# First stage of a two-block transformer kernel: modulation products ahead of the transpositions, and ring slots in the order of the loads

## The chip, the cores and the metric

One core of a Trainium2 chip runs the whole kernel. The metric is the device time of one execution in microseconds (us). TensorE is the matrix engine, VectorE (DVE) and ScalarE (ACT) are the vector and activation engines, GpSimd (POOL) is the general one, SyncE (SP) issues nearly all the loads. Each engine runs its own instructions in the order in which the program issues them, and waits on semaphores for the others.

## What is computed

Two transformer blocks on 256 tokens of 1024 features. What matters here is the beginning of the first block:

```
c_act = silu(c)
mod = c_act @ w_ada + b_ada                 # six vectors of 1024: sh_m, sc_m, gt_m, sh_f, sc_f, gt_f
h = rmsnorm(x, g) * (1 + sc_m) + sh_m
q, k, v, f_logit, u = split(h @ w_in)       # 512, 512, 512, 8 and 512 columns
log_f = log_sigmoid(f_logit + b_fgate)      # forget gates of 8 heads
x = x + gt_m * (concat(attention(q, k, v, log_f), pool(u)) @ w_out)
```

A router and 32 experts follow, of which each token uses two, and then a second block with other attention branches and a feed-forward layer.

## The kernel before

**Weights.** All weights stream from HBM as tiles of 1 MB (128 rows of 2048 float32) through a ring of eleven slots, 0 to 3 in one pool and 4 to 10 in another (four more come later for the experts). A list, `plan` (line 173), names the tiles in the order in which they are loaded, with the slot of each: `a` are the eight tiles of the first two modulation vectors, `b` and `c` eight each of the next two pairs, `i` the eight of `w_in`, `o` the four of `w_out`. SP issues the loads in that order; a load waits until the last reader of its slot's previous tile is done. The experts' tiles follow with a list of their own, `slots` (line 669), and the second block's with four slots in turn (line 679).

**Three-pass products.** The projections are computed in three passes of float32r: each half tile of weights is split into an upper part `whi` by ScalarE (line 69) and a lower part `wlo` by VectorE (line 70), the activations into `hT` and `hL`, and `mmx` (line 129) issues upper x upper, upper x lower and lower x upper: lines 133, 134, 135. `next2` (line 90) hands out a half and has the following ones split, two ahead; there are three buffers for them.

**The first stage, in the order of the code.** The norm of x: ScalarE squares and sums the rows (line 241), VectorE adds epsilon (242), ScalarE and VectorE take the inverse root (231 to 235), and the rows are scaled, one block of tokens by VectorE (247), one by ScalarE (249). TensorE transposes them, 16 times 128 x 128 (line 264), into four PSUM tiles `ptr`.

Then `ada_first` (line 273) makes the first two modulation vectors, 128 columns of both from each `a` tile. For tile d: 8 products of silu(c), padded to 32 columns, with the weights into `pa` (line 282), each on a quarter of the columns of the array; a copy into `mr` by ScalarE (284); a product with ones that sums over the partitions (288); the bias by VectorE into `modT` (289). The sum of tile d - 1 is issued behind the products of tile d. After each tile, the loop at line 348 forms the gain `A1` (349) and evacuates transposed column d into `hT` and `hL` with gain and shift: for even d VectorE makes `evt` (341), ScalarE `hT` (342) and GpSimd `hL` (343); for odd d ScalarE makes `evt` (334), VectorE both parts (335, 336).

After the eighth tile the first two halves of `i0` are split (351), the gate logits `pf` are formed in 24 passes (lines 364 to 366), and the key products follow: `feat` (381), four of them, each of 24 passes into `pp`. ScalarE and VectorE turn `pf` into cumulated log gates meanwhile (367 to 379). Behind the fourth key product comes the first step of `ada_next` (293), which makes the next modulation vectors tile by tile between the other products (`some`, line 389): four products on half of the columns (line 301) on TensorE, the other half on VectorE (303, 305). Values, queries, attention, pooling, output projection and router follow.

The order is written by hand: the program issues exactly in the order of the code.

## Time and profile before

| | us |
|---|---|
| three runs | 771.41, 778.97, 775.15 |
| median of the runs | 775.15 |
| span of the profiled execution, first to last instruction | 772.4 |
| TensorE busy in it | 695.8 (90%) |
| VectorE, ScalarE, GpSimd busy | 400.1, 305.2, 136.2 |
| DMA engines' mean | 269 GB/s over the span, 207.7 MB |

The profile gives no time of its own for the profiled execution besides the span. Times in the rows count from the span's first instruction. A row of a timeline stands for one instruction or for several alike in a row (x count): start, length, engine, line, operation, output and inputs, shape, and in brackets how long the engine was idle before and what ended that.

### The profile page before, as it was taken

What the parts mean: (1) busy time and instruction counts of PE and PEld (TensorE: products, weight loads), DVE (VectorE), ACT (ScalarE), POOL (GpSimd) and SP (SyncE); (2) the same over time, 40 slices, a digit from 0 to 9 for tenths busy, and PEclk for the clock granted to TensorE, in tenths of its full rate; (3) what the DMA queues carried; (4) which work ended last, traced back from release to release, by engine and by line L of the source; (5) the groups of instructions that cost most, each with busy time, mean ns of one, the idle gap of its engine ahead of it and who ended that gap; (6) DMA issues with size and microseconds to landing.
All of it is one profiled execution on the core that took longest, in us unless ns stands there. A gap on an engine that the chain in (4) does not pass through costs nothing.

```text
span 772.4 us, 12245 instructions
## 1 busy us (share of the span) xinstructions
PE 695.8 (90%) x4953; PEld 532.0 (69%) x4953; DVE 400.1 (52%) x661; ACT 305.2 (40%) x531; POOL 136.2 (18%) x137
## 2 busy tenths in 40 slices
PE   3899999679988778767889999999999999999996
PEld 2687777544433132231489999999989998989885
DVE  2666796511221020120598878677867654545545
ACT  3643543310010000000466456686555554545433
POOL 0102321000000000000322343221422540503201
PEclk9999999889998897998999999999999999999998
DMA  9998499849999999999855433335545555545511
GB/s 359 419 419 359 173 347 422 339 149 424 420 421 422 420 421 422 421 420 421 320 202 191 145 142 127 110 134 193 180 192 188 191 206 171 204 170 190 192 55 55
DMA packets 29726, 207.70 MB, mean 269 GB/s; under 512 B 3553, under 2 KB 3937, under 8 KB 4706
## 3 DMA queue, kind: packets, MB, share of 16 engines
q1 hardware_dynamic: 29520, 206.35, 68.2%
q8 instruction: 41, 0.67, 0.4%
q10 hardware_dynamic: 146, 0.53, 0.2%
q14 instruction: 19, 0.16, 0.1%
HBM read 205.81 MB, written 1.05 MB: 268 GB/s over the span
## 4 chain that ended last, share of the span: by engine, by line
PE 57%; DMA 19%; DVE 2%; issue 0%; DVEq 0%; ACT 0%; SPq 0%; ACTq 0%
DMA w<-in_w_gu 14%; PE pp L133 9%; PE pp L134 9%; PE pp L135 9%; PE fy L133 4%; PE fy L135 4%; PE fy L134 4%; DMA w<-in_w_in 3%; DMA w<-in_w_dn 3%; PE pgu L895 3%; PE pg L775 2%; PE pB L1226 2%; PE y L853 1%; PE pd L928 1%; PE pv L133 1%; PE pv L134 1%
## 5 line engine op out<-in xcount | busy, mean ns | idle before, releaser
L70 DVE TENSOR_TENSOR wlo<-w,whi 128x1024 fp32r<-128x1024 f32 x144 | 182.4, 1270 | 100.3 <-ACT whi L69 99.4
L69 ACT ACTIVATE whi<-w 128x1024 fp32r<-128x1024 f32 x146 | 153.4, 1055 | 81.5 <-PE fy L135 41.5
L134 PE MATMUL pp<-hL,whi 128*128 128x256 f32 x368 | 103.5, 281 | 2.6 <-DVE hL L882 2.6
L133 PE MATMUL pp<-hT,whi 128*128 128x256 f32 x368 | 105.5, 287 | 0.0
L895 PE MATMUL pgu<-w,hg 128*32 128x512 f32 x512 | 72.4, 672 | 35.7 <-DMA w<-in_w_gu 31.4
L135 PE MATMUL pp<-hT,wlo 128*128 128x256 f32 x368 | 103.5, 281 | 0.5 <-DVE wlo L70 0.5
L895 PEld LDWEIGHTS pgu<-w,hg 128*32 128x32 f32 x512 | 14.0, 115 | 88.6 <-issue 46.8
L133 PEld LDWEIGHTS pp<-hT,whi 128*128 128x128 f32 x368 | 69.6, 189 | 3.8 <-issue 3.0
L133 PE MATMUL pp<-nH,whi 128*128 128x256 f32 x256 | 71.8, 281 | 0.0
L134 PE MATMUL pp<-nL,whi 128*128 128x256 f32 x256 | 71.7, 280 | 0.0
L135 PE MATMUL pp<-nH,wlo 128*128 128x256 f32 x256 | 71.7, 280 | 0.0
L134 PEld LDWEIGHTS pp<-hL,whi 128*128 128x128 f32 x368 | 69.6, 189 | 2.8 <-POOL wlo L70 2.8
L135 PEld LDWEIGHTS pp<-hT,wlo 128*128 128x128 f32 x368 | 69.6, 189 | 0.7 <-DVE wlo L70 0.7
L903 DVE TENSOR_TENSOR act<-pgu,act 128x256 f32<-128x256 f32 x8 | 3.4, 425 | 121.3 <-ACT act L902 121.3
L1504 POOL TENSOR_TENSOR aL<-rs,aH 128x256 fp32r<-128x256 f32 x32 | 46.3, 1446 | 89.5 <-ACT aH L1503 83.4
L902 ACT ACTIVATE act<-pgu 128x256 f32<-128x256 f32 x8 | 3.1, 384 | 142.7 <-PE pgu L895 142.7
L133 PE MATMUL fy<-whi,aH 128*128 128x512 f32 x124 | 49.3, 398 | 0.0
L134 PE MATMUL fy<-wlo,aH 128*128 128x512 f32 x124 | 48.8, 394 | 0.0
L135 PE MATMUL fy<-whi,aL 128*128 128x512 f32 x124 | 48.8, 394 | 0.0
L133 PEld LDWEIGHTS pp<-nH,whi 128*128 128x128 f32 x256 | 48.2, 188 | 0.1
L134 PEld LDWEIGHTS pp<-nL,whi 128*128 128x128 f32 x256 | 48.2, 188 | 0.1
L135 PEld LDWEIGHTS pp<-nH,wlo 128*128 128x128 f32 x256 | 48.2, 188 | 0.0
(427 smaller groups left out, 1299.0 us busy)
## 6 DMA issues: line engine op xcount, KB each, us to landing
w<-in_w_gu SPq DMA_DIRECT2D x64, 1024.0 KB, 19.8
w<-in_w_dn SPq DMA_DIRECT2D x32, 1024.0 KB, 19.8
w<-in_w_ff SPq DMA_DIRECT2D x32, 1024.0 KB, 4.8
w<-in_w_in SPq DMA_DIRECT2D x30, 1024.0 KB, 5.0
w<-in_w_ada SPq DMA_DIRECT2D x24, 1024.0 KB, 11.7
w<-in_w_out SPq DMA_DIRECT2D x8, 1024.0 KB, 4.7
w<-in_w_o SPq DMA_DIRECT2D x4, 1024.0 KB, 4.8
xt<-in_x SPq DMA_DIRECT2D x1, 1024.0 KB, 5.1
```

The costliest lines, as they stand in the source:

```text
L69: nc.scalar.activation(hi, w, AF.Copy)
L70: low = lambda e, lo=lo, w=w, hi=hi: e.tensor_tensor(lo, w, hi.bitcast(F32), op=OP.subtract)
L133: mm(out_, l[0], r[0], start=start, stop=False)
L134: mm(out_, l[0], r[1], start=False, stop=False)
L135: mm(out_, l[1], r[0], start=False, stop=stop)
L775: mm(pg[:, d], xn[:, t, 512 * b + 128 * d:512 * b + 128 * d + 128], Pf[:, t], start=(t == 0), stop=(t == 1))
L853: mm(pacc[t][h], pw[g][:, 128 * t:128 * t + 128], o, start=False, stop=(g == 7))
L895: mm(pgu[32 * j:32 * j + 32], hg[g][:, k, 32 * j:32 * j + 32], w[:, 512 * j:512 * j + 512], start=(k == 0), stop=(k == 7))
L903: V.tensor_tensor(act, pgu[:, 256:512], act, op=OP.mult)
L928: mm(pd[32 * j:32 * j + 32], aT[:, f, 32 * j:32 * j + 32], w[:, 512 * j:512 * j + 512], start=(f == 0), stop=(f == 1))
L1226: mm(p[:, 4 * t + h], kt[:, h, 128 * t:128 * t + 128], qo[:, h, n * t:n * t + n], start=True, stop=True)
L1504: G.tensor_tensor(aL[:, f], s, aH[:, f].bitcast(F32), op=OP.subtract)
```

## The change

1. The order of the first stage. Products and sum of modulation tile 0 stand ahead of the norm of x, those of tile 1 behind it and ahead of the transpositions. For each tile the sum now stands behind its own products. Tiles 2 to 6 have three of the gate's passes between their products and their sum; the two halves of `i0` are split behind column 6; tile 7 has four of the first key product's eight steps there. Its other steps, the second key product and the last gate passes follow. The copy of tiles 0 and 1 goes from ScalarE to VectorE.
2. `pf` gets another PSUM buffer (that of the later scores), so that it can be accumulated over the rounds.
3. The order of the loads and the slots. `i` tiles alternate with `b` and `c` tiles, and tile n goes to slot n % 11; the experts' tiles go on in the same count, and the second block's take slots 0 to 3 in order.

The diff without the comments that it removes, without the removed `ada_first` and without the lines that only move:

```
-    plan = "a0-7 0-7 i0-4 0-4 b0-3 5-8 i5 9 b4 10 b5 5 i6 6 b6-7 7-8 c0 0 i7 1 c1-2 2-3 o0 8 c3 10 c4 5 c5 7 o1 0 c6 4 c7 2 o2 3 o3 10"
+    plan = "a0 a1 a2 a3 a4 a5 a6 i0 a7 i1 i2 b0 b1 i3 b2 b3 i4 b4 b5 i5 b6 b7 i6 c0 c1 i7 c2 c3 c4 c5 o0 c6 o1 c7 o2 o3".split()
...
+    for n, what in enumerate(plan):
         w, split = src[what[0]]
-        for i, slot in zip(span(what[1:]), span(where)):
-            st.add(w[i], split, slot)
+        st.add(w[int(what[1:])], split, n % 11)
...
+    def ada_tile(d):
+        w = st.next()
+        pa = ps.tile([128, 512], F32, name="pa", tag="m", bufs=2)
+        for k in (0, 2, 4, 6, 1, 3, 5, 7):
+            j = 32 * (k // 2)
+            mm(pa[j:j + 32, 0:256], cs[:, k, :], w[:, 256 * k:256 * k + 256], start=(k % 2 == 0), stop=(k % 2 == 1))
+        mr = q1.tile([128, 256], F32, name="mr", bufs=2)
+        if d < 2:
+            V.tensor_copy(mr, pa[:, 0:256])
+        else:
+            S.activation(mr, pa[:, 0:256], AF.Copy)
+        return pa, mr
+    def ada_sum(d, pa, mr):
+        for j in range(2):
+            mm(pa[:, 256 + j:257 + j], mr[:, 128 * j:128 * j + 128], ones, start=True, stop=True)
+        V.tensor_tensor(modT[:, 0:2, d], pa[:, 256:258], vec[:, V_BA + d:V_BA + 16:8], op=OP.add)
...
+    ada_sum(0, *ada_tile(0))
     wfh = q1.tile([128, 8, 8], F32R, name="wfh")
...
+    rms_scale(r1, xt, q1, xn)
+    for t in range(2):
+        scale_rows(xn, xt, r1, t)
...
-    for d, _ in enumerate(ada_first()):
+    pf = ps.tile([128, 256], F32, name="pf", tag="s", bufs=2)
+    def f_logits(k):
+        mmx(pf[0:8], (wfh[:, k], wfl[:, k]), (hT[:, k], hL[:, k]), start=(k == 0), stop=(k == 7))
+    def column(d):
         V.scalar_tensor_tensor(A1[:, d:d + 1], mod(1)[:, d:d + 1], 1.0, vec[:, V_GM + d:V_GM + d + 1], op0=OP.add, op1=OP.mult)
         evac_split(q1, xT[d], hT[:, d], hL[:, d], A1[:, d:d + 1], mod(0)[:, d:d + 1], v=d % 2)
+    ada_sum(1, *ada_tile(1))
+    xT = transposed(ps, "a", xn)
+    column(0)
+    column(1)
+    for d in range(2, 7):
+        t = ada_tile(d)
+        f_logits(d - 2)
+        ada_sum(d, *t)
+        column(d)
+    st.split_to(2)
+    t = ada_tile(7)
+    kw = [st.next2(False) for _ in range(2)]
+    kp = [ps.tile([128, 256], F32, name="pp", tag="a", bufs=4) for _ in range(2)]
+    def k_part(i, k0, k1):
+        for k in range(k0, k1):
+            mmx(kp[i], sub(kw[i], slice(None), slice(128 * k, 128 * k + 128)), (hT[:, k], hL[:, k]), start=(k == 0), stop=(k == 7))
+    k_part(0, 0, 4)
+    ada_sum(7, *t)
+    column(7)
+    k_part(0, 4, 7)
+    k_part(1, 0, 7)
+    for k in (5, 6, 7):
+        f_logits(k)
+    for i in range(2):
+        k_part(i, 7, 8)
     st.split_to(LOOK)
...
-    for i in range(4):
+    for i in range(2):
+        S.activation(kT[:, i], kp[i], AF.Copy)
+    for i in range(2, 4):
         feat(st.next2(), kT[:, i])
...
-    slots = [9, 5, 7, 6, 4, 2, 1, 8, 0, 3, 10]
+    slots = [(n_pre + n) % 11 for n in range(11)]
...
-            st.add(a[name][i], True, (0, 3, 2, 1)[n % 4])
+            st.add(a[name][i], True, n % 4)
```

TensorE's first instructions before (`pa` with `cs` are a modulation tile's products, `pa` with `ones` its sums, `ptr` the transpositions):

```order
L264 MATMUL ptr<-ident,xn 128x128 x16
L282 MATMUL pa<-w_169,cs 32x256 x8
L282 MATMUL pa<-w_182,cs 32x256 x8
L288 MATMUL pa<-ones,mr 128x1 x2
L282 MATMUL pa<-w_203,cs 32x256 x8
L288 MATMUL pa<-ones,mr 128x1 x2
```

and now:

```order
L265 MATMUL pa<-w_127,cs 32x256 x8
L275 MATMUL pa<-ones,mr 128x1 x2
L265 MATMUL pa<-w_166,cs 32x256 x8
L275 MATMUL pa<-ones,mr 128x1 x2
L252 MATMUL ptr<-ident,xn 128x128 x16
L265 MATMUL pa<-w_212,cs 32x256 x8
L133 MATMUL pf<-hT,wfh 8x256
L134 MATMUL pf<-hL,wfh 8x256
L135 MATMUL pf<-hT,wfl 8x256
L275 MATMUL pa<-ones,mr 128x1 x2
```

Two tiles moved ahead of the transpositions, and a tile's sums from behind the next tile's products to behind its own and three gate passes.

VectorE around the start of the norm, now (`ss` is the sum of squares to which epsilon is added; before, the row with `ss` stood directly behind the lower bounds `olb`):

```order
L216 TENSOR_SCALAR olb<-lb 128x4
L268 COPY mr<-pa 128x256
L276 TENSOR_TENSOR modT<-pa,vec 128x2
L311 CAST wfh<-wf 128x64
L312 TENSOR_TENSOR wfl<-wf,wfh 128x64
L236 TENSOR_SCALAR ss<-ss 128x2
```

Four instructions moved ahead of the norm's first one on VectorE.

ScalarE at the first split of weights, before (`hT` and `evt` belong to columns 6 and 7, `w_337` is tile `i0`):

```order
L284 ACTIVATE mr<-pa 128x256
L342 ACTIVATE hT<-evt 128x256
L334 ACTIVATE evt<-ptr,modT,A_166 128x256
L69 ACTIVATE whi<-w_337 128x1024 x2
L368 ACTIVATE fz<-pf,vec 8x256
```

and now (`w_332` is `i0`, `w_422` is `i1`):

```order
L329 ACTIVATE hT<-evt 128x256
L69 ACTIVATE whi<-w_332 128x1024 x2
L270 ACTIVATE mr<-pa 128x256
L321 ACTIVATE evt<-ptr,modT,A_162 128x256
L69 ACTIVATE whi<-w_422 128x1024 x2
L393 ACTIVATE fz<-pf,vec 8x256
```

The split of `i0` moved from behind the last column to between column 6 and the copy of the eighth modulation tile.

## Rows read from the trace of the kernel before

**Rows 1.** Busy time by stretch: start:end, length, engines' busy us, clock, DMA share, GB/s.
```profile
46.20:147.00 100.80, 98.91 (x737) 76.82 (x736) 69.48 (x114) 40.88 (x90) 19.07 (x38) 1.00 0.82 331
164.00:376.00 212.00, 172.06 (x1090) 65.50 (x1093) 34.58 (x82) 18.07 (x42) 0.00 (x0) 0.90 1.00 413
...
76.00:87.00 11.00, 11.00 (x90) 8.32 (x91) 9.40 (x21) 5.08 (x14) 5.16 (x13) 1.00 0.01 1
157.00:166.00 9.00, 4.71 (x34) 2.86 (x36) 2.29 (x7) 2.79 (x5) 0.00 (x0) 0.87 0.03 6
```
**Rows 2.** TensorE's waits from 10 to 170: total us, times, longest.
```profile
PE ptr L264 <- DVE xn L247: 12.1, 1, 12.1
PE pa L282 <- DVE modT L289: 1.8, 6, 0.3
```
**Rows 3.** Timeline of TensorE: transpositions, modulation products and sums.
```profile
12.15 3.86 PE L264 MATMUL ptr<-ident,xn 128*128 128x128 f32 x16 [12.15 <-DVE xn L247]
15.93 2.41 PE L282 MATMUL pa<-w,cs 128*32 128x256 f32 x32
20.20 0.61 PE L288 MATMUL pa<-ones,mr 128*128 128x1 f32 x4
21.13 1.07 PE L282 MATMUL pa<-w,cs 128*32 128x256 f32 x16 [0.32 <-DVE modT L289]
22.99 1.07 PE L282 MATMUL pa<-w,cs 128*32 128x256 f32 x16 [0.26 <-DVE modT L289]
...
134.87 1.03 PE L593 MATMUL pn<-ident,xt 128*128 128x128 f32 x8
```
**Rows 4.** Timeline of the other engines in a round.
```profile
20.91 0.16 DVE L289 TENSOR_TENSOR modT<-pa,vec 128x2 f32<-128x2 f32 x1 [0.99 <-PE pa L288]
21.11 0.16 DVE L349 SCALAR_TENSOR_TENSOR A<-modT,vec 128x1 f32<-128x1 f32 x1
22.33 0.38 ACT L284 ACTIVATE mr<-pa 128x256 f32<-128x256 f32 x1 [0.46 <-PE pa L282]
23.17 0.54 DVE L341 TENSOR_SCALAR evt<-ptr,A,modT 128x256 f32<-128x256 f32 x1
23.75 0.42 ACT L342 ACTIVATE hT<-evt 128x256 fp32r<-128x256 f32 x1 [1.03 <-DVE evt L341]
```
**Rows 5.** Timeline of gate passes, split and first key product, and of the first b product.
```profile
30.82 0.28 PE L133 MATMUL pf<-hT,wfh 128*8 128x256 f32 x1
30.93 0.28 PE L134 MATMUL pf<-hL,wfh 128*8 128x256 f32 x1
32.19 2.00 ACT L69 ACTIVATE whi<-w 128x1024 fp32r<-128x1024 f32 x2
33.50 2.36 DVE L70 TENSOR_TENSOR wlo<-w,whi 128x1024 fp32r<-128x1024 f32 x2
34.78 0.39 PE L135 MATMUL pp<-hT,wlo 128*128 128x256 f32 x1 [0.50 <-DVE wlo L70]
35.00 0.28 PE L133 MATMUL pp<-hT,whi 128*128 128x256 f32 x1
35.12 0.29 PE L134 MATMUL pp<-hL,whi 128*128 128x256 f32 x1
...
46.24 0.64 PE L301 MATMUL pa<-w,cs 128*32 128x256 f32 x8
```
**Rows 6.** Loads of the first and the ninth tile: issue, and its time to landing.
```profile
2.86 4.89 SPq L50 DMA_DIRECT2D w<-in_w_ada  x8
DMA to landing us min/median/max: 6.5/6.5/6.5
17.55 0.33 SPq L50 DMA_DIRECT2D w<-in_w_in  x1
DMA to landing us min/median/max: 12.7/12.7/12.7
```
**Rows 7.** Timeline of VectorE at the start of the norm.
```profile
10.08 0.17 DVE L242 TENSOR_SCALAR ss<-ss 128x2 f32<-128x2 f32 x1 [1.30 <-ACT xn L241]
```

More of the change, by code (lines that the diff above doesn't have):

```diff
@@ L172, in body @@
     st.slots.update({i: ring if i < 4 else ring2 for i in range(11)})
-    plan = "a0-7 0-7 i0-4 0-4 b0-3 5-8 i5 9 b4 10 b5 5 i6 6 b6-7 7-8 c0 0 i7 1 c1-2 2-3 o0 8 c3 10 c4 5 c5 7 o1 0 c6 4 c7 2 o2 3 o3 10"
+    plan = "a0 a1 a2 a3 a4 a5 a6 i0 a7 i1 i2 b0 b1 i3 b2 b3 i4 b4 b5 i5 b6 b7 i6 c0 c1 i7 c2 c3 c4 c5 o0 c6 o1 c7 o2 o3".split()
     src = {"a": (a["w_ada"][0], 0), "b": (a["w_ada"][1], 0), "c": (a["w_ada"][2], 0), "i": (a["w_in"], 1), "o": (a["w_out"], 1)}
-    def span(x):
-        lo, _, hi = x.partition("-")
-        return range(int(lo), int(hi or lo) + 1)
-    plan = plan.split()
-    for what, where in zip(plan[::2], plan[1::2]):
+    for n, what in enumerate(plan):
         w, split = src[what[0]]
-        for i, slot in zip(span(what[1:]), span(where)):
-            st.add(w[i], split, slot)
+        st.add(w[int(what[1:])], split, n % 11)
     ones = cp.tile([128, 1], F32, name="ones")
@@ L249, in scale_rows @@
             S.activation(dst[:, t], src[:, t], AF.Copy, scale=r[:, t:t + 1])
-    xn = cp.tile([128, 2, 1024], F32, name="xn")
-    r1 = q1.tile([128, 2], F32, name="r1")
-    rms_scale(r1, xt, q1, xn)
-    for t in range(2):
-        scale_rows(xn, xt, r1, t)
     def transposed(ps, tag, src):
@@ L266, in transposed @@
         return r
-    xT = transposed(ps, "a", xn)
     modT = cp.tile([128, 6, 8], F32, name="modT")
-    def ada_first():
-        last = None
-        for d in range(9):
-            if d < 8:
-                w = st.next()
-                pa = ps.tile([128, 512], F32, name="pa", tag="m", bufs=2)
-                for k in (0, 2, 4, 6, 1, 3, 5, 7):
-                    j = 32 * (k // 2)
-                    mm(pa[j:j + 32, 0:256], cs[:, k, :], w[:, 256 * k:256 * k + 256], start=(k % 2 == 0), stop=(k % 2 == 1))
-                mr = q1.tile([128, 256], F32, name="mr", bufs=2)
-                S.activation(mr, pa[:, 0:256], AF.Copy)
-            if last:
-                pl, ml = last
-                for j in range(2):
-                    mm(pl[:, 256 + j:257 + j], ml[:, 128 * j:128 * j + 128], ones, start=True, stop=True)
-                V.tensor_tensor(modT[:, 0:2, d - 1], pl[:, 256:258], vec[:, V_BA + d - 1:V_BA + 16:8], op=OP.add)
-                yield
-            last = pa, mr
+    def ada_tile(d):
[14 more added lines that the diff above has]
+        V.tensor_tensor(modT[:, 0:2, d], pa[:, 256:258], vec[:, V_BA + d:V_BA + 16:8], op=OP.add)
     def ada_next(g):
@@ L343, in evac_split @@
             G.tensor_tensor(lo, t, hi.bitcast(F32), op=OP.subtract)
+    xn = cp.tile([128, 2, 1024], F32, name="xn")
+    r1 = q1.tile([128, 2], F32, name="r1")
+    rms_scale(r1, xt, q1, xn)
+    for t in range(2):
+        scale_rows(xn, xt, r1, t)
     A1 = q1.tile([128, 8], F32, name="A1")
@@ L362, in body @@
     catL = q1.tile([128, 8, 256], F32R, name="catL")
-    pf = ps.tile([128, 256], F32, name="pf", tag="a", bufs=4)
-    for k in range(8):
-        mmx(pf[0:8], (wfh[:, k], wfl[:, k]), (hT[:, k], hL[:, k]), start=(k == 0), stop=(k == 7))
     fz = q1.tile([8, 256], F32, name="fz", tag="mr", bufs=2)
```

## The prediction

> **What bounds the kernel now.** I read the table of busy time by stretch first, then TensorE's waits, then the timeline of the first 47 us, then the loads. The table by stretch [rows 1] shows four stages with three different limits. From 46.2 to 147 us TensorE is busy 98.91 of 100.80 us: whatever comes to it earlier or later by some time ends earlier or later by that time. Then the router runs, a chain of small steps, until about 164. From 164 to 376 the 16 DMA engines are busy all the time (share 1.00, 413 GB/s): the experts run at the pace of their weights. What follows (not shown here) is TensorE again. Two rows of the same group tell how the stages hang together. From 76 to 87 the DMA engines do nothing (share 0.01) while TensorE is busy 11.00 of 11.00 us, so in the first stage the loads are ahead of their use. From 157 to 166 they do nothing again (0.03): all fifteen slots that can be filled ahead for the experts are full, and the next load waits until TensorE frees one. So the bandwidth-bound stage starts when TensorE starts it, and a shift of the first stage goes through to the end of the kernel undiminished, in either direction.
>
> Thus only one thing is to be worked out: when TensorE reaches a point from which the order is the same in both kernels. I take the first product with the b weights (line 301), after all four key products: 46.24 us [rows 5].
>
> TensorE's waits say what there is to gain before that point: 12.1 us ahead of the first transposition, 1.8 us in six pieces between modulation products [rows 2], 0.5 us ahead of the first key product [rows 5]. The first is the tempting one. Its end is not all gain: the first modulation weights land at 9.4 us (issued at 2.86, 6.5 us to landing) [rows 6].
>
> **The change part by part.** The work on TensorE is the same: 8 modulation products, 8 pairs of sums over partitions, 16 transpositions, 24 gate passes, the key products. What changes is who waits in front of whom.
>
> *Two modulation products ahead of the transpositions.* A tile's product takes 1.07 us and its two sums 0.61 us at full pace [rows 3]. Before about 17 us TensorE runs at about half: 16 transpositions take 3.86 us, while eight take 1.03 us later [rows 3]. At half pace the first tile's product is done at 9.4 + 2.1 = 11.5. Its copy is now VectorE's; no row shows that copy, so I bound it by ScalarE's 0.38 and by VectorE's 0.54 for a tile of this shape with a scale and bias [rows 4], and take 0.45: 12.1 with 0.1 on each crossing (the sum ends at 20.81, the next step starts at 20.91) [rows 3, 4]. The sums take 1.2 at half pace: 13.3. Now comes the catch: VectorE runs in order, and the norm of x stands behind this sum. The add of epsilon (line 242, before at 10.08) [rows 7] comes after the modulation add and the two small casts of the gate weights, at about 14.0 instead of 10.08, so the rows of x are scaled at 16.1 where it was 12.1. VectorE then copies the second product (0.45), TensorE sums it (0.9 at half pace), and only then transposes: start 17.4, before 12.15. That is 5.3 us later, for two tiles of work (about 3.4 us at full pace) done ahead. The third modulation product starts after 16 transpositions, at 20.6 if they run at half pace (16 x 0.21 = 3.4), at 18.9 if the clock has risen by then (1.7).
>
> *Five rounds in which the sum no longer lags.* Before, the sum of tile d - 1 stood behind the product of tile d, so that ScalarE's copy had a whole product as cover; a round took 22.99 - 21.13 = 1.86 us [rows 3]. Now the sum of tile d stands directly behind its own product with three gate passes (0.34 us) between. A round is product 1.07, crossing 0.1, copy 0.38, crossing 0.1, sum 0.45 until the next product may start: 2.1 us. After an even column it is more, for ScalarE also writes hT: from the sum's start 0.61, crossing 0.1, modT 0.16, A 0.16, evt 0.54, hT 0.42 and small gaps make 2.1 us [rows 3, 4], while the next copy wants ScalarE at 0.45 + 1.07 + 0.1 = 1.6; it starts 0.45 late, and that round takes 2.55. Five rounds: 2.1 + 2.55 + 2.1 + 2.55 + 2.1 = 11.4. The weights do not set this pace: at 420 GB/s a 1 MB tile takes 2.5 us, tile 6 lands long before its round, and tile 7, now one place later in the queue, lands at 30.2 (the ninth megabyte of weights did so before: 17.55 + 12.7) [rows 1, 6]. The eighth product may start at 18.9 + 11.4 = 30.3, or 32.0.
>
> *Key products in between.* The two halves of the first key tile are split on ScalarE and VectorE, 2.00 and 2.36 us for two [rows 5]. They are issued behind column 6 and ahead of the eighth tile's copy. ScalarE ends column 6 at 1.67 us after the eighth product may start; the upper part takes 1.05, the lower part 1.23 more: the third pass of the first key product can run at + 4.05. TensorE has 1.0 of product and two passes (0.24) until then and stands still for about 2.8 us, where it stood for 0.5 before [rows 5]. The remaining 46 passes at 0.12, one pair of sums (0.44) and nine gate passes at 0.11 (1.0) make 6.96, and so both products end at + 11.0. The eighth column's own way (ScalarE's copy, sum, evt, hT, hL) is hidden behind these passes; without that cover it would cost about 2 us. Products three and four (48 x 0.12 = 5.76) bring the b product to + 16.8.
>
> The sum: 18.9 + 11.4 + 16.8 = 47.1 with an early rise of the clock, 20.6 + 11.4 + 16.8 = 48.8 with a late one; before 46.24. So the change costs 0.85 to 2.55 us. I take the middle, + 1.7, since no row decides where the clock rises.
>
> *Slots and the order of loads.* With b and i tiles in alternation the i tiles land up to 10 us later than before (`i4` has four tiles more ahead of it, at 2.5 us), and the c and o tiles earlier. I cost both at nothing: TensorE's unbroken work covers it [rows 1], and counted at 2.5 us a tile, the later i tiles still land about 5 us ahead of their split (an estimate). If that cover were gone, one late tile would cost at most its 2.5 us. SP issues the same loads; a tile of the second block gets another slot, freed some microseconds later but still ahead of its turn in the queue: 0.
>
> The profiled execution's span is 772.4; the median of three runs is 775.15. The shift does not depend on what lies between them, so I add it to the median: 775.15 + 1.7 = 776.9 (the span would be 774.1).
>
> **The rivals.** *First, not slower.* If the rounds keep the old pace, the two tiles done ahead pay. With an early clock the change breaks even when 18.9 + 5 P + 16.8 = 46.24, that is at a round of P = 2.1 us; at the old 1.9 it gains 1.0 us: 774.1. For it speaks that ScalarE is little used between 17 and 31; against it that its copy needs 0.1 + 0.38 + 0.1 in each round and the cover is three passes. As worked out above, the rounds after odd columns come out at just that limit, the others above.
>
> *Second, slower than forecast.* TensorE stays at its lower level past the transpositions. By the row alone the rise came 4 to 5 us after TensorE's first product at 12.15, which is also 4 to 5 us after the beginning of its first unbroken work [rows 3]; the changed kernel pulls these apart, with the first product at 9.4 and unbroken work only from 16.6. Counted from the latter plus a round at half pace, the sum becomes about + 4.2: 779.3. It decides when the rise comes after 21 us. The Trainium skill ("TensorE: Matmul & The Clock Gate", Part 1) says that the low level is the default, that activity releases it, and that the moment is not tied to the kernel's start. By that rule scattered products would count for less than I give them in the middle, and the time would lie at or above 777.7, the late end of my sum; this trace, with its single unbroken start, agrees with either reading.
>
> *Third, the loads decide.* If the new order of slots is what matters, the idle DMA stretch at 76 to 87 closes and the kernel gains nothing from it, since nobody waits there: 775.2. Against a gain speaks that the only waits on loads are in the expert stage, whose start TensorE sets.
>
> **How the numbers follow.** Chances: 0.6 for the forecast (0.85 to 2.55 slower), 0.17 for the first rival, 0.15 for the second, 0.03 for the third, 0.05 for what I do not see. Runs of the kernel before lie within 3.8 us of their median; for a median of a few I allow 3 (an estimate). The furthest gain is TensorE without a break from the landing of tile 7: 30.2 + 1.07 + 5.76 + 0.44 + 1.0 + 5.76 = 44.2 at the b product, 2.0 earlier. So the range goes from 775.15 - 2.0 - 3 = 770.1 to 775.15 + 4.2 + 3 = 782.3. A measurement of this kernel tells about 1% (7.75 us) from no change. No case above reaches that by itself; slower gets 0.07 for the second rival with an unseen stall, faster 0.04, no change 0.89.
>
> **What would show it.** In the profile after: the first modulation product at 9.5 and the transpositions not at 12 but at 17; rounds of 2.1 and 2.5 us in alternation, ended by ScalarE's copy; a wait of some 2.8 us ahead of the third pass of the first key product on the lower part of the weights; the first b product between 47 and 49 us; no idle DMA at 76 to 87 and the same idle stretch ahead of the experts; from there on everything later by the same 1 to 3 us. I am wrong if the b product comes before 46 us, if TensorE waits for a load in the first stage, or if the difference grows or shrinks after 50 us.

## The result, and the profile after

The changed kernel takes 781.42 us in the median of 11 runs (777.70 to 784.33); 11 runs of the kernel before have a median of 773.42 (770.97 to 778.97). The ratio is 1.0091, interval [1.0072, 1.011]: 7 us slower by the ratio (0.0091 x 773.42), 8 by the medians, where 1.7 was forecast. The time lies inside the range given, near its upper end, and the sign was right; the size was not. The profiled execution took 779.16, its span is 777.3. (One execution each of e7 and c6 and two of e15, below, were longer than their kernel's others by hundreds of us; medians and counts are given without them.)

What bounds the kernel after? First the table by stretch, as [rows 1]; the sixth column is the granted clock, 1.00 for the upper level (2.4 GHz) and 0.50 for the lower (1.2 GHz). The bounds of the last three rows are set where the clock changes.

```profile
46.20:147.00 100.80, 99.30 (x732) 77.06 (x730) 72.68 (x120) 43.19 (x94) 19.01 (x38) 0.98 0.83 325
164.00:376.00 212.00, 167.31 (x1095) 66.67 (x1093) 35.99 (x87) 18.85 (x44) 0.00 (x0) 0.93 0.97 401
...
76.00:87.00 11.00, 11.00 (x88) 8.45 (x88) 8.11 (x18) 3.97 (x13) 5.12 (x11) 1.00 0.83 308
157.00:166.00 9.00, 5.55 (x36) 5.47 (x36) 4.98 (x27) 0.54 (x3) 0.00 (x0) 0.62 0.63 265
...
21.20:34.70 13.50, 10.89 (x121) 5.92 (x117) 5.12 (x18) 5.49 (x12) 2.53 (x6) 1.00 1.02 416
34.70:41.60 6.90, 6.15 (x29) 6.06 (x29) 3.77 (x7) 2.25 (x4) 0.00 (x0) 0.51 1.02 418
72.30:75.70 3.40, 3.40 (x19) 2.19 (x19) 1.98 (x4) 2.59 (x9) 0.00 (x0) 0.50 1.01 414
```

The reader is to see two rows that have no counterpart before, the last two: TensorE is busy nearly all the time, yet at half its clock, from 34.7 to 41.6 and again from 72.3 to 75.7. In the kernel before the column reads 1.00 from 17.0 to 46.2, and so it does from there to 147 [rows 1]. (Ahead of its first rise the column shows 1.00 too, though the transpositions run at half pace; that rise is read from durations.) The idle stretch of the DMA engines at 76 to 87 is closed (0.83 against 0.01), and nobody gains by it, since TensorE is busy 11.00 of 11.00 there in both.

TensorE's waits up to 60 us, as [rows 2]:

```profile
PE pa L265 <- DMA w<-in_w_ada: 8.8, 1, 8.8
PE pp L133 <- ACT whi L69: 1.6, 1, 1.6
PE pa L275 <- DVE mr L268: 1.6, 2, 1.0
PE pp L135 <- DVE wlo L70: 0.8, 1, 0.8
PE pa L275 <- ACT mr L270: 0.8, 2, 0.4
```

The wait of 12.1 for the norm has become one of 8.8 for the first load; the six small waits on `modT` are gone; new are 1.6 on VectorE's copies of tiles 0 and 1, 0.8 on ScalarE's copies in two of the rounds, and 1.6 on the upper part of the first key tile; the wait on its lower part has grown from 0.5 to 0.8. The same in TensorE's timeline, as [rows 3, 5] (lines of the changed kernel: 265 modulation products, 275 sums, 252 transpositions, 133 to 135 passes, 286 first b product, 470 first scores):

```profile
8.84 1.94 PE L265 MATMUL pa<-w,cs 128*32 128x256 f32 x16 [8.84 <-DMA w<-in_w_ada]
16.08 3.65 PE L252 MATMUL ptr<-ident,xn 128*128 128x128 f32 x16
19.66 1.74 PE L265 MATMUL pa<-w,cs 128*32 128x256 f32 x16
...
24.34 0.61 PE L275 MATMUL pa<-ones,mr 128*128 128x1 f32 x4 [0.38 <-ACT mr L270]
...
31.64 1.07 PE L265 MATMUL pa<-w,cs 128*32 128x256 f32 x16
34.28 0.39 PE L133 MATMUL pp<-hT,whi 128*128 128x256 f32 x1 [1.56 <-ACT whi L69]
35.54 0.58 PE L135 MATMUL pp<-hT,wlo 128*128 128x256 f32 x1 [0.75 <-DVE wlo L70]
36.13 0.42 PE L134 MATMUL pp<-hL,whi 128*128 128x256 f32 x1
36.35 0.42 PE L135 MATMUL pp<-hT,wlo 128*128 128x256 f32 x1
...
51.13 0.64 PE L286 MATMUL pa<-w,cs 128*32 128x256 f32 x8
...
52.30 0.38 PE L134 MATMUL pv<-wlo,hT 128*128 128x256 f32 x1 [0.21 <-DVE wlo L70]
...
69.57 0.48 PE L470 MATMUL s<-kT,qT 64*128 64x128 f32 x2 [0.47 <-ACT qT L410]
```

and the first scores in the kernel before:

```profile
64.20 0.48 PE L443 MATMUL s<-kT,qT 64*128 64x128 f32 x2 [0.48 <-ACT qT L385]
```

Behind the wait the key passes follow each other every 0.22 us (36.13 to 36.35), where they did every 0.12 before [rows 5]. The b product stands at 51.13, before at 46.24: + 4.9. Followed product by product, the shift is 5.4 at the first scores (69.57 against 64.20; the 0.5 arises at the first value product, which waits for its lower weights at 52.30), 6.8 behind the second stretch at the lower level, and still 6.8 at the first expert product (170.68 against 163.90). In the expert stage it shrinks to 5 in this execution (the first product behind it: 381.83 against 376.71).

The other engines, at the norm and around that wait, as [rows 5, 7]:

```profile
12.80 0.16 DVE L236 TENSOR_SCALAR ss<-ss 128x2 f32<-128x2 f32 x1
...
32.86 0.42 ACT L329 ACTIVATE hT<-evt 128x256 fp32r<-128x256 f32 x1 [1.81 <-DVE evt L328]
33.19 1.99 ACT L69 ACTIVATE whi<-w 128x1024 fp32r<-128x1024 f32 x2
34.26 2.36 DVE L70 TENSOR_TENSOR wlo<-w,whi 128x1024 fp32r<-128x1024 f32 x2 [1.43 <-ACT whi L69]
```

ScalarE stood for 1.81 us ahead of the split: column 6 stands in front of it in its order, and waits for VectorE.

### The profile page after: what moved, and what is told of

Same layout as the page of the kernel before. It is cut to its first block, busy times and chain, and to the rows that moved or that the text cites. A ratio compares the mean times of both kernels' runs of the same rounds, so it can differ in the third digit from the quotient of the medians.

```text
span 777.3 us, 12247 instructions
## 1 busy us (share of the span) xinstructions
PE 700.5 (90%) x4953; PEld 536.9 (69%) x4953; DVE 399.3 (51%) x663; ACT 303.2 (39%) x529; POOL 136.1 (18%) x137
## 3 DMA queue, kind: packets, MB, share of 16 engines
HBM read 205.81 MB, written 1.05 MB: 266 GB/s over the span
## 4 chain that ended last, share of the span: by engine, by line
PE 53%; DMA 23%; DVE 2%; issue 0%; ACT 0%; DVEq 0%; SPq 0%; ACTq 0%
DMA w<-in_w_gu 15%; PE pp L133 9%; PE pp L134 9%; PE pp L135 9%; DMA w<-in_w_dn 8%; PE fy L133 4%; PE fy L135 4%; PE fy L134 4%; PE pgu L922 2%; PE pB L1253 2%; PE pv L133 1%; PE pv L134 1%; PE pv L135 1%; PE acc L134 1%; PE acc L135 1%; PE acc L133 1%
## 5 line engine op out<-in xcount | busy, mean ns | idle before, releaser
L69 ACT ACTIVATE whi<-w 128x1024 fp32r<-128x1024 f32 x146 | 153.2, 1053 | 86.3 <-PE fy L135 41.6
L133 PE MATMUL pp<-hT,whi 128*128 128x256 f32 x368 | 107.4, 292 | 1.6 <-ACT whi L69 1.6
L134 PEld LDWEIGHTS pp<-hL,whi 128*128 128x128 f32 x368 | 71.2, 193 | 2.7 <-POOL wlo L70 2.7
L134 PE MATMUL pp<-nL,whi 128*128 128x256 f32 x256 | 71.8, 280 | 0.0
L135 PE MATMUL pp<-nH,wlo 128*128 128x256 f32 x256 | 71.8, 280 | 0.0
```

The source lines that it names most:

```text
L69: nc.scalar.activation(hi, w, AF.Copy)
L133: mm(out_, l[0], r[0], start=start, stop=False)
L134: mm(out_, l[0], r[1], start=False, stop=False)
L135: mm(out_, l[1], r[0], start=False, stop=stop)
```

## The experiments

The theory: the changed order costs some 2.5 us by its waits, and the rest because TensorE's clock falls behind the wait ahead of the key products. The rivals: the waits alone, and the new order of the loads. The kernels ran in five groups, each on one chip beside runs of the kernel before, with which their ratios are formed: e1 to e4; e5, e7, e8 and e11; e12 to e15; c1 to c4; c5 and c6.

**Loads alone, order alone.** e1 is the kernel before with only the new `plan`, `slots` and `n % 4`; e2 is the changed kernel with the old ones.

```
# e1, in the kernel before (e2 is the reverse edit in the changed kernel)
-    plan = "a0-7 0-7 i0-4 0-4 b0-3 5-8 ..."
+    plan = "a0 a1 a2 a3 a4 a5 a6 i0 a7 i1 i2 b0 ...".split()
...
-    slots = [9, 5, 7, 6, 4, 2, 1, 8, 0, 3, 10]
+    slots = [(n_pre + n) % 11 for n in range(11)]
...
-            st.add(a[name][i], True, (0, 3, 2, 1)[n % 4])
+            st.add(a[name][i], True, n % 4)
```

> The kernel before with only the new order of loads and the new slots (first stage, experts, second block); the order of the work is the old one. Theory clock (the order of the work makes TensorE wait ahead of the key products, and the fall of its clock behind that wait costs more than the wait) and rival waits (only the waiting itself costs): both expect no change, within 1.5 us of before, first b product at 46 to 46.5 us. Rival loads (a part of the loss is in the loads and slots): 2 us or more slower.

Measured: 777.11 (12 runs; before beside them 773.24), ratio 1.0045 [1.0027, 1.0062]: under the old order of work the new loads cost 3.5 us, which both the theory and the waits alone had excluded. TensorE's timeline and the clock of e1:

```profile
27.25 0.60 PE L281 MATMUL pa<-ones,mr 128*128 128x1 f32 x4
30.02 1.08 PE L275 MATMUL pa<-w,cs 128*32 128x256 f32 x8 [2.16 <-DMA w<-in_w_ada]
```

```profile
29.80:36.50 6.70, 6.48 (x38) 4.21 (x39) 2.66 (x8) 2.90 (x5) 1.08 (x4) 0.50 1.02 423
70.80:74.10 3.30, 3.30 (x19) 2.18 (x19) 1.98 (x4) 2.52 (x9) 0.00 (x0) 0.50 1.00 412
```

The eighth modulation tile, now behind `i0`, lands 2.2 us later; the old rounds are at it earlier and wait 2.16 us, and the clock falls in that wait. The b product stands at 50.05, + 3.8. So a second, quite different wait of 2 us is followed by two such falls.

> The changed kernel with the old order of loads and the old slots. Clock and waits: 6 to 9 us slower than before, as the changed kernel. Loads: 2 us or more faster than the changed kernel.

Measured: 779.23 (6 runs), 1.0076 [1.0046, 1.0106], overlapping the changed kernel's interval; the same waits of 1.6 and 0.8, the same falls (0.52 from 35.8 to 42.5, 0.54 from 73.4 to 76.7), and the b product at 51.74, no earlier than with the new loads (51.13). Under the new order of work no cost of the loads can be told, since the rounds come to the eighth tile only at 31.64; the two intervals still leave room for some us.

**The wait shortened, the wait filled.** e3 splits the first half of `i0` one round earlier. e4 leaves the wait and puts useless products into it.

```
# e3, in the changed kernel
     for d in range(2, 7):
         t = ada_tile(d)
+        if d == 6:
+            st.split_to(1)
         f_logits(d - 2)
# e4, in the changed kernel
+    dm = ps.tile([128, 256], F32, name="dm", tag="s", bufs=2)
+    for i in range(24):
+        mm(dm, hT[:, i % 4, 0:128], hT[:, i % 4], start=True, stop=True)
     k_part(0, 0, 4)
```

> The changed kernel with the first half of i0 split right behind the copy of the seventh modulation tile instead of behind column 6. The wait ahead of the first key product's passes (1.56 and 0.75 us) should shrink to 0.5 or less. Clock: TensorE keeps its upper level between 31 and 46 us, the first b product comes at 46 to 47.5 instead of 51.1, the whole is 1 to 4 us slower than before. Waits: only the wait goes, b product at 49 or later, 4 to 6 us slower than before.

Measured: 777.07 (12), 1.0042 [1.0024, 1.006]. The wait on the key tile is down to 0.17, but ScalarE's copy for the eighth sum is now late by 1.6 us; the lower level lasts from 36.6 to 39.9, half as long, and again from 70.7 to 74.0. The b product comes at 49.01, where the waits alone expected 49 or later and the clock 46 to 47.5, while the time is what the clock expected: since the wait was moved and not taken away, this run does not part the two.

> The changed kernel with 24 further products of 256 columns into an unused PSUM tile between the eighth modulation product and the first key product; nobody reads them. They take about 2.9 us and lie in the time in which TensorE waits for the split. Clock: the upper level is kept, the first b product comes at 48 to 49 instead of 51.1, the whole is 2 to 4 us faster than the changed kernel. Waits: no gain, b product at 51 to 51.5, time as the changed kernel or up to 0.5 us more.

Measured: 776.72 (12), 1.0050 [1.0029, 1.0072]. Stretches of e4, from the filled wait on:

```profile
31.40:36.20 4.80, 4.80 (x48) 4.20 (x49) 2.86 (x6) 2.58 (x4) 1.08 (x4) 1.00 1.05 426
36.20:46.20 10.00, 10.00 (x87) 9.77 (x86) 4.59 (x9) 4.82 (x10) 0.00 (x0) 1.00 1.01 415
46.20:147.00 100.80, 99.25 (x739) 77.25 (x739) 72.59 (x119) 41.76 (x89) 19.07 (x38) 1.00 0.83 326
```

No stretch below 1.00: with 24 products more the kernel is 3 to 5 us faster than the changed one (by the ratios, by the medians). The b product stands at + 2.6, though the filler ran 0.5 us longer than the wait. The waits alone expected no gain, b product at 51 or later; the clock expected 48 to 49, and 48.87 was measured.

**Is it this wait only?** e5 undoes the two tiles ahead of the transpositions. e7 holds ScalarE for 2 us in the kernel *before*; e8 does so and fills TensorE's time. e11 is to rid the changed kernel of both kinds of wait. The removed lines of e5 and the tail of e11 are left out below.

```
# e5, in the changed kernel: tiles 0 and 1 behind transposed()
...
+    xT = transposed(ps, "a", xn)
+    ada_sum(0, *ada_tile(0))
     ada_sum(1, *ada_tile(1))
-    xT = transposed(ps, "a", xn)
# e7, in the kernel before
+    for t in range(2):
+        S.activation(xn[:, t], xt[:, t], AF.Copy)
     st.split_to(LOOK)
# e8: e7, and behind the gate passes 18 products as in e4
...
+    for i in range(18):
+        mm(dm, hT[:, i % 4, 0:128], hT[:, i % 4], start=True, stop=True)
# e11, in the changed kernel
+    last = None
     for d in range(2, 7):
         t = ada_tile(d)
-        f_logits(d - 2)
-        ada_sum(d, *t)
-        column(d)
+        if d == 6:
+            st.split_to(1)
+        if last:
+            ada_sum(d - 1, *last)
+            column(d - 1)
+        f_logits(d - 2)
+        last = t
...
```

> The changed kernel with one part undone: modulation tiles 0 and 1 stand behind the transpositions again; sums directly behind their products, gate passes in the rounds, the split behind column 6 and the new loads stay. If the late rise of the clock (my second rival) is part of the loss: transpositions at 12.2 and the rise at about 17 again, the b product 1.5 to 2.5 us earlier than in the changed kernel, 777 to 779.5. If the two tiles done ahead pay for themselves: three more rounds' time behind the transpositions, the b product later than in the changed kernel by 1 us or more, 782 or more. If only the waits ahead of the key products and the fall of the clock behind them count: these waits (1.56 and 0.75) and the fall at about 35 stay, b product within 1 us of the changed kernel's 51.13, 780 to 782.

Measured: 784.09, 6 runs between 775.44 and 787.02; ratio 1.0118 [1.0075, 1.016]. The time fits the second expectation, its reason does not. The stretch of its profiled execution that explains it:

```profile
21.20:48.40 27.20, 26.04 (x165) 16.23 (x158) 10.80 (x28) 8.83 (x17) 3.26 (x7) 0.51 1.02 418
```

The clock rose ahead of 18 (0.95 from 17.8 to 21.1) and was gone again at 21.2, in the first rounds, for 27 us; the b product stands at 57.52. One program, one chip: 775.44 at a mean granted clock of 0.971 in one execution, 787.02 at 0.949 in another. I read the falls as draws, whose odds and places depend on the order; what decides a single one, no run shows.

> The kernel before, with two more copies of 128x1024 on ScalarE ahead of the split of the first key tile (their result is not read); nothing else is changed, so TensorE stands about 1.9 us longer ahead of the first key product, in much the pattern of the changed kernel (1.5 for the upper part, 1.0 for the lower). Theory of the waits alone: everything behind is later by 1.9, b product at 48.1, end + 1.9, ratio 1.0025. Theory of the clock: the granted clock falls to its lower level behind the wait, key passes 0.21 instead of 0.12 us apart, b product + 4 to + 5; a second fall near the scores at 70 to 76 us, + 5 to + 6.5 behind it, and + 3.5 to + 5 at the end, ratio 1.0045 to 1.0065.

Measured: 776.05 (9), 1.0032 [1.0014, 1.0049], between the two theories. In the profiled execution the clock was lower from 30.9 to 34.2 already, so during the gate passes, ahead of the wait that the hold makes and behind rounds that this kernel shares with the kernel before:

```profile
27.50:30.80 3.30, 2.95 (x37) 1.97 (x30) 1.40 (x7) 1.73 (x4) 0.73 (x1) 1.00 1.02 399
30.90:34.20 3.30, 3.30 (x17) 2.06 (x16) 1.86 (x5) 2.86 (x5) 1.08 (x4) 0.50 1.00 415
```

So the trace gives no ground to put this fall down to the hold, and e7 does not test whether a wait brings one on; c6 below shows that the old order of work can fall at that place without a hold. The fall cost little, as TensorE would have stood for the hold anyway: b product + 1.66. A second one came at the scores (0.50 from 68.5 to 71.8).

> The same hold, and 18 products of 128x256 between the gate passes and the first key product, into a PSUM tile that nobody reads (2.1 us of useless work in the time in which TensorE stood). Theory of the waits alone: as without them, + 1.9 throughout, the same time as the run with the hold alone. Theory of the clock: no fall, b product + 1.9 to 2.1, no second fall, end + 1 to + 2, ratio about 1.002: faster than the hold alone by 2 to 4 us, with 18 products more.

Measured: 774.10 (14), 0.9997 [0.9976, 1.0017]. 2.0 us faster than the hold alone by the medians, as the clock theory had it (the intervals just overlap); b product at the same + 1.65, which the end does not show (+ 1 to + 2 was expected, the interval reaches + 1.3). The profiled execution is that kernel's longest, 782.13, and has a fall at the scores (0.51 from 68.5 to 75.2); the others were not profiled.

> A repair of the changed kernel: sums of tiles 2 to 6 lag one round again, and the first half of the first key tile is split right behind the copy of the seventh modulation tile. TensorE then has no wait over 0.5 us between the transpositions and the b product except, at most, for the landing of the eighth tile at 29.9. Theory of the clock: no fall before 150 us, b product at 44.5 to 46.2 (the furthest gain was 44.2), end 0 to 2 us ahead of the kernel before, ratio 0.9975 to 1.0. If the order of the head itself costs (tiles ahead, late rise at 19 to 21), the b product stays behind 47 even without waits: ratio 1.001 to 1.004.

Measured: 776.03 (12), 1.0032 [1.0015, 1.005], not the 0 to 2 us ahead of the kernel before that were expected. TensorE's timeline shows why:

```profile
28.20 0.61 PE L275 MATMUL pa<-ones,mr 128*128 128x1 f32 x4
31.11 1.07 PE L265 MATMUL pa<-w,cs 128*32 128x256 f32 x16 [1.52 <-DVE modT L276]
```

The early split on ScalarE delays column 5 and with it `modT`; a wait of 1.52 stands in the last round instead, and the clock is at 0.50 from 32.9 to 36.2, behind that wait; no second fall follows. The b product stands at + 1.0 (47.26).

**All waits filled.** The filler is now 128 x 128 in bfloat16 (`idle(n)`). e12: four in each round of the changed kernel, 40 ahead of the key products. e13: four a round and eight ahead of the key products in the kernel before. e14: e13 and 120 ahead of the transpositions. e15: e12 and all waits from 2 us on.

```
+    def idle(n):
+        for i in range(n):
+            mm(dm[:, 0:128], identb, identb, start=True, stop=True)
```

> The changed kernel with useless products of 128x128 in bfloat16 into a PSUM tile that nobody reads: four ahead of the sums of each round from the third on, 40 ahead of the first key product. Theory: the loss is an order cost of about 2.6 us at the b product plus what falls of the granted clock cost, which differ from execution to execution and strike where TensorE works thinly. Then here no fall between the rise and 69 us, b product + 2 to + 3.5, and the median + 1.5 to + 3 over the kernel before, ratio 1.002 to 1.004. Rival, waits alone (the falls are not worth more in one kernel than in the other): about the changed kernel's time, 1.008.

Measured: 780.65 (6), 1.0102 [1.007, 1.0134], against a trace that shows no fall and + 2.1 up to 154 us. The difference lies behind it, at the branch ahead of the experts:

```profile
169.09 3.64 PE L930 MATMUL pgu<-w,hg 128*32 128x512 f32 x16 [7.03 <-issue]
```

The first expert product is waited for 7.03 us, in the changed kernel 3.96, in the kernel before 4.28, in the other whole kernels traced 3.2 to 4.5. That is 3 us more, and with what came before it the product stands at + 5.2 (169.09 against 163.90). What causes it was not tried. This execution is the kernel's fastest (778.02); whether the others wait as long, and where the median's 7 us arise, is not shown. So the expectation of 1.5 to 3 failed in the whole kernel; the first stage by itself is measured with c3.

> The control: the kernel before with four such products behind each round's sums and eight ahead of the first key product, all in time in which TensorE stood. If executions of the kernel before also lose time to falls in the first stage now and then: 0 to 1.5 us faster, ratio 0.998 to 1.0. If they do not: 1.0 to 1.001.

Measured: 773.12 (12), 0.9997 [0.9978, 1.0015]. Within 2 us either way: no sign that the median execution of the kernel before has much to lose.

> The control with 120 more of these products ahead of the transpositions, from about 2 us on, where TensorE stood until 12.1. If the clock rises with them, ahead of 12: transpositions in 2 us instead of 3.86, the third to seventh modulation products up to 1.8 us earlier, until the eighth waits for its tile, which landed at 27.71 (its product ran at 28.71): b product 1.0 earlier than in the control, ratio 0.998 to 0.9995. If the rise does not come with useless products, or the first stage is bound by its loads anyway: as the control.

Measured: 772.46 (12), 0.9990 [0.9964, 1.0016]. The timeline is as expected: 16 transpositions in 2.25 instead of 3.86, the b product at 45.24, against 46.24 in the kernel before and 46.61 in e13.

```profile
11.88 2.25 PE L264 MATMUL ptr<-ident,xn 128*128 128x128 f32 x16 [1.41 <-DVE xn L247]
...
45.24 0.64 PE L309 MATMUL pa<-w,cs 128*32 128x256 f32 x8
```

One us is too little to be told in the whole kernel's time.

> The changed kernel filled as in e12 and in all waits from 2 us on. If the late rise (19 to 21) costs what the transpositions lose (3.65 at 16.08, 1.8 at the upper level): third modulation product at 17.9 instead of 19.66, b product 1.5 to 2 us earlier than in e12, that is + 0.3 to + 1.5 over the kernel before, ratio 1.0 to 1.002; what is then left against the warmed kernel before is the order's own price, 1 to 2.5 us. If the rise does not matter: as e12.

Measured: 776.93 (12), 1.0038 [1.0017, 1.0058], above the 1.0 to 1.002 that were expected and below e12. There is no trace of an ordinary execution, so c5 has to tell where the time lies.

**The first stage alone, in many executions.** One profiled execution cannot tell chance from a lasting loss, and the expert stage differs by some us from execution to execution (against the kernel before, e14 stands at - 1.5 where it begins and at - 4.2 behind it, e8 at + 4.4 and + 6.2). So six kernels were ended behind the first stage (the "cut" kernels of the expectations). All have this edit:

```
     p1a.close()
+    nc.sync.dma_start(out.rearrange("(t p) d -> p t d", p=128), xt)
+    return
```

> The kernel before, ended behind the first stage (residual and second norm; router, experts and second block are left out, and the rows are written out as they stand). The expert stage, whose length differs by some us from execution to execution, is gone, so each time tells the first stage of one execution. About 155 to 160 us. If falls of the granted clock are draws that the kernel before mostly escapes: most times within 0.5 us, a few later by 1.5 to 3.

> The changed kernel, ended at the same place. Theory (order 2.6 at the b product, the rest falls of the clock that this order meets in most executions): median + 5 to + 7 against the cut kernel before, times spread over several us with a lowest near + 2.5, and the later ones with the lower mean clock. Rival (the loss is waits alone, and the profiled execution's falls were chance): median near + 2.6, spread as before. Second rival (the loss arises behind the first stage, at the router or the experts): + 2 or less.

> The changed kernel with 60 useless bfloat16 products in its rounds and ahead of the first key product, ended at the same place. Its profiled execution had no fall and stood at + 2.1 at 147 us, but the full kernel's median was + 7 over before. If the median execution does fall (the filler works only sometimes): + 4 or more here, spread out. If its first stage is well and the rest was lost later (router, experts): + 2 to + 2.5 here, narrow.

> The changed kernel with 24 useless products of 128x256 in float32r ahead of the first key product, ended at the same place. Theory: no fall in most executions, + 2.6 to + 3.1 against the cut kernel before, 2 to 4 us faster than the cut changed kernel. Waits alone: as the cut changed kernel.

> The cut changed kernel with the useless products of e15 in all of TensorE's waits from 2 us on. If the late rise of the clock (19.8 to 22 in all runs of this order so far, ahead of it the transpositions in 3.65 us) is the larger part of the + 2.5 that the thick one keeps: third modulation product at 17.9 instead of 19.7, b product + 0.3 to + 1.2 over the kernel before, and 153.2 to 154.2. If the waits of the rounds and the key products alone make it: 155 to 155.6, as c3.

> The cut kernel before with the useless products of e14 (120 ahead of the transpositions, four a round, eight ahead of the key products): rise at 5 to 9, b product - 1.0, 151.8 against the 152.84 of the cut kernel before. The difference to c5 is what the order itself costs with the clock at its upper level throughout in both.

Measured, each execution with its mean granted clock:

| kernel | us (clock) |
|---|---|
| c1, before | 152.07 (0.995), 152.33 (0.995), 153.34 (0.999), 154.29 (0.982) |
| c2, after | 159.40 (0.965), 160.00 (0.965), 160.55 (0.967), 160.65 (0.949) |
| c3, after, e12's filler | 154.88 (0.998), 155.35 (0.999), 155.36 (0.999), 155.49 (0.998), 159.53 (0.970) |
| c4, after, e4's filler | 154.84 (0.996), 155.44 (0.999), 155.63 (0.997), 157.51 (0.987), 157.62 (0.987), 158.19 (0.987) |
| c5, after, filled from 2 us on | 153.63 (0.998), 153.69 (1.000), 153.91 (1.000), 155.22 (0.989), 155.33 (0.987) |
| c6, before, filled from 2 us on | 151.77 (0.997), 151.81 (1.000), 151.95 (0.995), 153.32 (0.987), 155.24 (0.975) |

The whole loss is here: medians 152.84 and 160.28, + 7.4. All four executions of the changed order have a lowered clock; the best, 159.40, is 3.9 us above four of the five of the filled kernel c3. Of c4's six, three kept the clock, and three, with a mean of 0.987, are 2.2 longer by the medians; in the one that was profiled the first fall, ahead of 48, did not come, only one from 70.0 to 73.3. Filling does not rule falls out: one execution of c3 and two each of c5 and c6 have a lowered clock. (The record of the clock begins at its first rise, so a late rise does not lower this mean; 153.34 at 0.999 may be one, which is not shown.) The profiled executions of c2 and c3, stretches and b product:

```profile
35.70:42.30 6.60, 6.51 (x30) 6.51 (x31) 3.44 (x7) 1.51 (x2) 0.00 (x0) 0.50 1.00 412
73.20:76.50 3.30, 3.30 (x19) 2.49 (x20) 2.46 (x5) 2.17 (x7) 0.00 (x0) 0.50 1.04 395
...
51.51 0.64 PE L286 MATMUL pa<-w,cs 128*32 128x256 f32 x8
```

```profile
20.30:46.20 25.90, 25.43 (x287) 20.19 (x280) 11.74 (x28) 11.88 (x23) 2.52 (x6) 1.00 1.02 417
...
47.90 0.64 PE L286 MATMUL pa<-w,cs 128*32 128x256 f32 x8
```

And c5, with the clock at its upper level from 5.4 on:

```profile
14.92 1.92 PE L252 MATMUL ptr<-ident,xn 128*128 128x128 f32 x16
...
29.99 1.07 PE L265 MATMUL pa<-w,cs 128*32 128x256 f32 x16 [1.86 <-DMA w<-in_w_ada]
...
46.29 0.64 PE L286 MATMUL pa<-w,cs 128*32 128x256 f32 x8
```

The transpositions take 1.92 instead of 3.65, and now the eighth tile's load is waited for, as in e1: the new place of that tile is hidden only as long as the rounds are late. The filled old order waits for that tile too, but runs its product at 28.09, 1.9 earlier. The profiled execution of c6 (155.24) then falls, with the filler in place, behind waits of 0.39, 0.65 and 1.05 for loads:

```profile
28.09 1.07 PE L289 MATMUL pa<-w,cs 128*32 128x256 f32 x16 [1.05 <-DMA w<-in_w_ada]
...
29.90:33.20 3.30, 3.30 (x20) 2.47 (x20) 2.28 (x7) 2.30 (x4) 1.07 (x4) 0.51 1.03 425
67.40:70.70 3.30, 3.30 (x18) 1.77 (x17) 1.98 (x4) 2.28 (x9) 0.00 (x0) 0.50 1.01 422
```

So the loss splits, by single executions that kept the clock: the order with its loads, with the clock up early in both, 153.69 - 151.81 = 1.9; the late rise in the changed order 155.36 - 153.69 = 1.7 (the old order's rise costs it 152.33 - 151.81 = 0.5); the falls 160.28 - 155.36 = 4.9. Together 1.9 + 1.7 - 0.5 + 4.9 = 8.0, which is 160.28 against 152.33; as each term is a difference to the next kernel, they must add up, and each stands by its own evidence only.

The falls' 4.9 agrees with the rows of c2: 9.9 us at half the clock with TensorE busy for 9.81 of them are 4.9 us of work lost (an estimate). The 1.7 and the 0.5 compare two chips; for the 1.7 the traces agree, with the b product at 47.90 in c3 and 46.29 in c5 and the same time from there on to the router's logits (101.2 and 101.1), while the 0.5 is within the differences of c1's own executions. And the 1.9 is not the order of the work by itself: it is as much as the eighth tile lands later by its new place in the list of loads (29.99 against 28.09). A filled changed kernel with the old loads was not run.

## Why the prediction was wrong

**What bounds the kernel.** Right that only the b product's time matters up to the router, and that TensorE decides it. "A shift of the first stage goes through to the end of the kernel undiminished" failed: + 4.9 at the b product became + 5.4 by a wait at the value products and + 6.8 by the second fall, and the expert stage takes or gives some us in each execution. I had named growth or shrinkage behind 50 us as a sign that I am wrong, and it was.

**Two tiles ahead.** Right in its mechanism: the norm's step on VectorE moved from 10.08 [rows 7] to 12.80 (14.0 forecast), the transpositions from 12.15 to 16.08 (17.4). They ran at half pace to the end (3.65), so the third product came at 19.66, between my 18.9 and 20.6. c5 against c3 puts the price of this late rise at 1.6 to 1.7 and shows that a rise ahead of it is to be had.

**Five rounds.** Right: 2.43 and 2.17 in alternation (forecast 2.55 and 2.1), the longer ones ended by ScalarE's copy as said; the first took 2.8, as the clock rose inside it. Sum 31.64 - 19.66 = 12.0, forecast 11.4.

**Key products in between.** The third pass came at 31.64 + 3.90, forecast + 4.05; TensorE stood 1.56 + 0.75 = 2.3 us ahead of it, forecast 2.8. Then the step that failed: "the remaining 46 passes at 0.12 [...] and so both products end at + 11.0", with the b product at + 16.8. It came at + 19.5, since the passes ran at 0.22 up to 41.6. I had priced the wait as time in which TensorE stands, and its passes behind it at the upper clock, without a row of passes behind such a wait. c3, without the fall, goes from the same third pass (35.17) to the b product (47.90) in 12.73; from the 35.54 of the changed kernel that would be 48.3, so + 2.0, inside the 0.85 to 2.55 of the sum. The sum was right for a clock that stays up; the missing term is what the falls cost, 4.9 us in the kernels ended behind the first stage.

**Slots and loads at nothing.** Not contradicted beside the new order (e2), but for a reason that I gave only in part: e1 shows the eighth tile's new place at 2.2 us of wait and 3.5 us of time under the old order. It is covered by the late rise and the slower rounds (the product ran at 31.64, 1.4 after the 30.2 at which I forecast the landing), not by unbroken work, and with an early rise it is paid for (c5).

**The rivals.** The first fell: in the kernels ended behind the first stage no execution of the changed order came within 5 us of one of the old order (c1, c2). The second, the late rise, was the right place to look and the wrong event: the rise at 21 cost what the sum had for it; what I did not list is a fall after a rise. The third, that the loads decide and the time stays at 775.2, fell: the idle stretch of the DMA engines closed and nobody gained, as it said, but the order of the work cost 7 us beside it (e2).

**The range.** It is luck that it holds the time. It was set from the median of the first three runs, 775.15; from the 773.42 of eleven, the same bounds end at 780.6. Its largest loss, 4.2, was worked out for a whole round at half pace behind a late rise, and the first round took 2.8; for falls it has nothing.

The Trainium skill ("TensorE: Matmul & The Clock Gate", Part 1), which I cited for the rise alone, says that the low level is the default and that the same kernel changes level at other points from execution to execution, as the gate does not start with the kernel. By that rule a wait amid work can cost more than itself, and by different amounts; the runs agree: 775.44 and 787.02 for one program (e5).

**What stays open.** What makes the clock fall in one execution and not in another, as in c6 with most waits filled; why the second fall, at the first scores (beginning between 67 and 79 us), follows in each profiled execution with a first fall but e11, and comes in e8 and c4 without one; how the 1.9 parts into order and loads; and the 3 us at the branch of e12.

**A version better than both?** Filling TensorE's waits from 2 us on brings the old order's b product 1.0 us earlier (e14), and its first stage is 0.5 us shorter where the clock stays up (c6, 151.81 against 152.33, on two chips); in the whole kernel it is 0.9990 [0.9964, 1.0016], no difference that can be told. Nothing tried here beats the kernel before measurably.

## What to carry to other kernels

A wait of TensorE amid work is to be priced twice: by its length, and by what a fall of the granted clock behind it would cost if it comes (here 2 us of wait, 5 us of loss); read the clock column of the stretch behind every wait that an edit makes. To tell the two apart, fill the wait with useless products: if the kernel becomes faster with more work, it was the clock. (The filler does not hold the clock in each execution, and whole kernels with it can lose the gain elsewhere, as e12 did.) And where a time is a mixture of draws, end the kernel behind the stage in question and list its executions one by one; one trace shows one draw.

## What the runs showed of the hardware that was not expected

Useless products on an idle TensorE are worth time: 24 of them made the changed kernel 3 to 5 us faster, and with 66 or 120 small ones from 2 us on the clock was at its upper level by 6 (c5, c6, e14), where the first real work otherwise saw it at 16 to 22.

The clock can stay low over a stretch in which TensorE is busy nearly all the time: in e5 at 0.51 from 21.2 to 48.4, with TensorE busy 26.04 of 27.20 us, and that execution took 785.67 where another of the same program took 775.44.
